# A two-layer diffusion trunk on one core: the retention branch's own products by seven block products, and its last gate put behind the first Fourier projection

## Chip, cores and metric

One core of one Trainium2 chip. The metric is the device time of one launch in microseconds (us), lower is better.

## What is computed

The reference runs two layers over 640 tokens (512 noisy ones and 128 of a prompt, each group with its own modulation). A layer projects the normalised input once, has three branches (retention, latent attention, Fourier mixing), and merges them:

```
h = rms_norm(x, norm_g) * (1 + scale) + shift
rq, rk, rv, rz, q_lat, kv_lat, k_r, mz, fu, fz, gl = split(h @ w_in)
...
branches = [o_r * silu(rz), o_m * silu(mz), o_f * silu(fz)]      # each 512 wide
proj     = branches[n] @ w_branch[n]                             # 512 x 1024, n = 0, 1, 2
merged   = sum over n of proj[n] * sigmoid(gl[n])                # gl: 3 x 1024 columns of h @ w_in
x        = x + gate * (merged @ w_out)
```

Every f32 operand is kept as two tiles, a rounded high part and the rest, and each product is three matmuls (high x high, high x low, low x high).

## The kernel before

Channels lie on the partitions and the 640 tokens on the free axis, in two halves of 320. PE is TensorE, DVE VectorE, ACT ScalarE, POOL GpSimd; SP issues most DMAs. Instructions are written in program order, and a scheduler sorts those of each engine into a fixed queue by its own estimate of times; each engine then works through its queue in order.

A layer has these stages: attention; retention (`retention`, four heads, whose `Filler` computes silu of the gate columns between the heads' own matmuls); Fourier mixing (`fourier`); the merge; the output projection. Three things matter here.

**Retention's last gate.** For each head `norm(hd)` transposes the head's output (L787), takes means and variances on DVE (L789, L790), a power on POOL, one more DVE operation (L795), and five scalings on ACT (L798). `gate(hd)` has the silu values finished by the filler (`rz.finish`, matmuls L319 in the one `fill` bank of PSUM, emptied by ACT's tanh L321 and DVE's L322), transposes back (L807) and multiplies on DVE (L808). `norm(3)` and `gate(3)` are the last lines of `retention`. `fourier` then starts with `sums(k)` (DVE and ACT prepare the sums of hidden columns) and `project(0)`, the first Fourier projection, 120 matmuls of 256 columns (L85 to L87).

**The merge.** Three passes n = 0, 1, 2 work on latent attention (`omt`), retention (`ort`) and Fourier (`ort` again, loaded from `ofd` in pass 1). A pass has four blocks i of 256 output channels. A block first computes the gate's columns with `seven` (a 2 x 2 block product by seven products in place of eight; 84 matmuls of 320 columns), then the branch's own product. In passes 0 and 2 that is `seven` again (42 matmuls). In pass 1 it is `four`, the plain product: 48 matmuls. `seven` needs its operand as seven sums, the parts p0 to p6, which `branch_sums` makes on DVE and ACT: eleven DVE operations of 640 elements a pass, four of them sums made in place in the source, seven of them the low half of a part, in tiles `bq0` to `bq9` and `bql`. `four` needs only the four quarters as they are (`branch_split`, `bq0` to `bq7`). The weights likewise: `br_weights` makes sums of them (`wsums`), `br_plain` does not. The last two products of a `seven` (`rest`) are issued inside the next one (`flush`).

**Buffers.** The tiles `bq0` to `bq9` and `bql` have one buffer each, and `wh` and `wl` have four. A pass can fill a part's tile only when the pass before has used it for the last time.

Of the kernel before, what the change touches and what calls it, by code (L numbers as in the profile page):

```python
# [9 lines left out]
F32R = mybir.dt.float32r  # L10
# [20 lines left out]
def build(nc, tc, A, O):  # L31
# [38 lines left out]
    def h2(sb):  # L70
        return sb.rearrange("p (h n) -> p h n", h=2)
# [590 lines left out]
    def retention(l, rp, orr, spare):  # L662
# [139 lines left out]
        def gate(hd):  # L802
            nn = outp[hd]
            z = rz.finish(hd + 1)
            pt = big()
            for t in range(NT):
                PE.transpose(pt[:, t * P:(t + 1) * P], nn[:, t * P:(t + 1) * P], ident)  # L807
            DVE.scalar_tensor_tensor(orr[hd], pt[:, :TT], 0.5, z, op0=ALU.mult, op1=ALU.mult)  # L808
# [23 lines left out]
        for p in todo:  # L832
            mix(*p)
        norm(3)
        gate(3)


    def fourier(l, fp, of, sums, wgp):
        def table(name, src, a, n):
            raw = fp.tile([P, a, n], F32, name="traw", tag="traw", bufs=1)  # L840
            nc.sync.dma_start(raw, src)
# [68 lines left out]
        def prompt_t(g):  # L910
# [4 lines left out]
            split(upc[0][:, g, :], upc[1][:, g, :], Up[:, 0:P], scale=1.0 / 128)  # L915
            split(ups[0][:, g, :], ups[1][:, g, :], Up[:, P:256], scale=-1.0 / 128)

        for k in range(4):
            sums(k)
        project(0)  # L920
        teo = [table(f"te{i}", A["k_dft"][i].rearrange("(a p) n -> p a n", p=P), 2, 256) for i in range(2)]
        tp_ = table("tpr", A["k_dftp"].unsqueeze(1), 1, 256)
        cf = table("tcf", A["k_dftf"].unsqueeze(1), 1, 256)
# [135 lines left out]
        g = lambda w, i: (w[0][:, s[i]], w[1][:, s[i]])  # L1059
        return g(w1, 0), g(w1, 3), g(w1, 1), g(w1, 2), g(w2, 0), g(w2, 1), g(w2, 2)  # L1060

    def br_plain(l, idx, c0):
        r = wraw(rows(A["w_branch"][l, idx], 0, 4, c0, 256), 4, 256)
        w = wtiles(4, 256)
        split(w[0], w[1], r, leng=DVE)
        return w

    def branch_split(gp, src):
        for w in range(4):
            hi, lo = (gp.tile([P, 2, 320], F32R, name=f"bq{2 * w + i}", tag=f"bq{2 * w + i}", bufs=1) for i in range(2))  # L1070
            split(hi, lo, h2(src[:, w, :]))
            yield hi, lo

    def four(ws, xs, y2, ms, ps, tick, mid=None, fin=None):
        for j in range(2):
            for h, hs in enumerate(HALF):
                A = bank()
                for k in range(4):
                    for i, (u, v) in enumerate(PASSES):
                        PE.matmul(A, ws[u][:, k, j * P:(j + 1) * P], xs[k][v][:, h, :], start=(k == 0 and i == 0),  # L1080
                                  stop=(k == 3 and i == 2))
                if not (j or h):
                    flush()
                    if mid:
                        mid()
                DVE.scalar_tensor_tensor(ps[j][:, hs], y2[j][:, hs], 1.0, A, op0=ALU.add, op1=ALU.mult)
                tick(3 * h)
                if fin:
                    DVE.tensor_tensor(ms[j][:, hs], ms[j][:, hs], ps[j][:, hs], op=ALU.add)
                    fin(j, hs)  # L1090
            if not fin:
                DVE.tensor_tensor(ms[j], ms[j], ps[j], op=ALU.add)

    tail = []

    def flush():
# [90 lines left out]
    for l in range(DEPTH):  # L1187
# [8 lines left out]
        orr = [ort[:, w, :] for w in range(4)]  # L1196
        off = [oft[:, w, :] for w in range(4)]
        with ExitStack() as s:
            retention(l, pool(s, f"re{l}"), orr, off)
        s3 = ExitStack()  # L1200
        hqp = pool(s3, f"hq{l}")
        wgp = pool(s3, f"wg{l}")
        with ExitStack() as sx:
            sums, close, hq = hidden_sums(hqp, pool(sx, f"hx{l}"), off)
            with ExitStack() as s:
                w0, gated = fourier(l, pool(s, f"fo{l}"), off, sums, wgp)
            close()
        ofd = dp.tile([P, 4, TT], F32, name=f"ofd{l}")
        for w in range(2):
# [4 lines left out]
        with ExitStack() as s:  # L1214
# [57 lines left out]
            for n, (idx, src, tmp) in enumerate(((1, omt, None), (0, ort, om), (2, ort, om))):  # L1272
                if n:
                    flush()
                parts = branch_split(gp, src) if n == 1 else branch_sums(gp, src, bql)
                np_ = 4 if n == 1 else 7
                bq = []
                for i in range(4):
                    if n and i % 2 == 0:
                        y2 = tmp[2:4]  # L1280
                    else:
                        y2 = [fl.tile([P, TT], F32, name="tg", tag="th", bufs=2) for _ in range(2)]
                    seven(gl_weights(wgp, l, C_GL + D * idx + 256 * i), hq, *y2, *gates(y2, n, bq, parts, np_))
                    if n == 2 and i == 3:
                        merge(0, 4)
                    if i == 0:
                        flush()
                        bq += list(parts)
                        if n == 1:
                            for w in range(4):  # L1290
                                nc.sync.dma_start(ort[:, w, :], ofd[:, w, :])
                    ms = [mg[2 * i], mg[2 * i + 1]]
                    ps = tmp[0:2] if n else ms
                    if n == 1:
                        ends = (lambda: merge(4, 6), lambda j, hs: merge(6 + j, 7 + j, hs)) if (n, i) == (2, 3) else ()
                        four(br_plain(l, idx, 256 * i), bq, y2, ms, ps, lambda i: next(steps, None) if i else None, *ends)
                    else:
                        seven(br_weights(wgp, l, idx, 256 * i), bq, *ps, *products(y2, n, ms, ps))
            merge(4, 6)
            flush()  # L1300
            merge(6, NK)
# [158 lines left out]
```

## Time and profile before

| | |
|---|---|
| median of 3 runs | 1472.1 us (1469.72 to 1475.49) |
| the profiled execution | 1475.04 us |
| its span on the core | 1473.3 us |
| PE busy | 96% of the span, 9793 matmuls |
| DVE busy | 70% |
| ACT, POOL busy | 51%, 16% |
| stage with the merge, layer 0 and 1 | 428 to 697 us and 1148 to 1401 us |

Times in the trace count from the start of the span. A matmul's duration overlaps the next one's, so what one costs is the distance between starts, or a stretch divided by its count. DVE's operations overlap a little too. A row with `[0.55 <-DVE th L322]` says that the engine was idle for 0.55 us before this instruction, until that operation ended.

### The profile page before, as it was taken

To read this page: it belongs to the slowest core of one execution; us is meant where nothing else is said; L and a number is where in the kernel's file an instruction comes from. 1 tells how busy PE (TensorE), PEld (TensorE's weight loads), DVE (VectorE), ACT (ScalarE), POOL (GpSimd) and SP (SyncE) were. 2 spreads that over 40 slices of the span, in tenths; PEclk is the share of its full clock that TensorE was granted. 3 is DMA by queue.
4 is the path that set the end of the run, shared out by engine and by line. 5 is a ranking of instruction groups with operands and counts; after the bars stand their busy time and mean duration, and the time that the engine had idled before them with its cause. 6 is when DMAs were issued, how large, how long until landed. Compare 5 with 4: busy or idle time off the path is not lost.

```text
span 1473.3 us, 25184 instructions
## 1 busy us (share of the span) xinstructions
PE 1411.6 (96%) x9793; PEld 1345.2 (91%) x9793; DVE 1025.5 (70%) x1896; ACT 756.2 (51%) x1607; POOL 239.1 (16%) x227
## 2 busy tenths in 40 slices
PE   6999999999999999999999999999999999999997
PEld 4989989988988989999999899899889899999997
DVE  5367776666887686698573777765759778779843
ACT  5546666544545453455354566664545445445542
POOL 1220000301102211122312100021110112112240
PEclk9999999999999999999999999999999999999999
DMA  9520003331325474233532100042222433323342
GB/s 317 179 76 1 15 16 98 102 84 33 94 90 176 130 221 129 57 85 92 166 101 84 33 15 16 15 138 77 73 73 65 146 108 104 94 80 86 90 125 87
DMA packets 175847, 138.91 MB, mean 94 GB/s; under 512 B 8304, under 2 KB 168688, under 8 KB 175728
## 3 DMA queue, kind: packets, MB, share of 16 engines
q1 hardware_dynamic: 157680, 120.16, 28.1%
q10 hardware_dynamic: 18048, 17.15, 3.7%
q8 instruction: 77, 1.26, 0.4%
q14 instruction: 42, 0.34, 0.1%
HBM read 125.98 MB, written 11.30 MB: 93 GB/s over the span
## 4 chain that ended last, share of the span: by engine, by line
PE 74%; DVE 12%; DMA 5%; ACT 4%; issue 4%; POOL 1%; SPq 0%; POOLq 0%; ACTq 0%; DVEq 0%
PE bank L1109 25%; PE sm L85 6%; PE sm L87 5%; PE sm L86 5%; PE big L269 4%; PE bank L1080 4%; PE big L513 4%; PE fill L319 3%; PE sm L319 3%; PE sm L534 2%; PE sm L526 2%; DVE wl L74 2%; PE fill L187 2%; DMA raw<-in_w_in 1%; PE big L411 1%
## 5 line engine op out<-in xcount | busy, mean ns | idle before, releaser
L74 DVE TENSOR_TENSOR wl<-raw,wh 128x1024 fp32r<-128x1024 f32 (+5 forms) x146 | 153.8, 1055 | 87.3 <-ACT wh L78 39.0
L78 ACT CAST wh<-raw 128x1024 fp32r<-128x1024 f32 (+5 forms) x126 | 104.7, 833 | 86.2 <-DMA raw<-in_w_in 27.9
L1109 PE MATMUL bank<-hh,wh 128*128 128x320 f32 x416 | 130.0, 315 | 5.5 <-ACT tg L1125 4.4
L85 PE MATMUL sm<-wh,hh 128*128 128x256 f32 (+2 forms) x456 | 134.2, 295 | 0.5 <-DVE vl L74 0.5
L86 PE MATMUL sm<-wl,hh 128*128 128x256 f32 (+2 forms) x456 | 133.8, 294 | 0.0
L87 PE MATMUL sm<-wh,hl 128*128 128x256 f32 (+2 forms) x456 | 132.6, 294 | 0.0
L1109 PE MATMUL bank<-hl,wh 128*128 128x320 f32 x416 | 128.6, 310 | 0.0
L1109 PE MATMUL bank<-hh,wl 128*128 128x320 f32 x416 | 127.1, 311 | 0.0
L74 POOL TENSOR_TENSOR wl<-raw,wh 128x1024 fp32r<-128x1024 f32 (+1 forms) x32 | 66.4, 2075 | 294.9 <-ACT wh L78 215.7
L74 POOL TENSOR_TENSOR wl<-st,wh 128x512 fp32r<-128x512 f32 x26 | 38.0, 1463 | 328.8 <-ACT wh L78 328.8
L85 PEld LDWEIGHTS sm<-wh,hh 128*128 128x128 f32 x456 | 87.8, 193 | 2.2 <-issue 0.8
L1109 PEld LDWEIGHTS bank<-hh,wh 128*128 128x128 f32 x416 | 78.3, 188 | 11.9 <-ACT tg L1125 5.2
L86 PEld LDWEIGHTS sm<-wl,hh 128*128 128x128 f32 x456 | 87.8, 193 | 0.1
L87 PEld LDWEIGHTS sm<-wh,hl 128*128 128x128 f32 x456 | 87.4, 192 | 0.4 <-issue 0.4
L1109 PEld LDWEIGHTS bank<-hl,wh 128*128 128x128 f32 x416 | 78.5, 189 | 0.0
L1109 PEld LDWEIGHTS bank<-hh,wl 128*128 128x128 f32 x416 | 78.0, 189 | 0.0
L74 DVE TENSOR_TENSOR ptl<-sm,pth 128x384 fp32r<-128x384 f32 x128 | 67.2, 549 | 13.9 <-ACT pth L78 12.9
L1109 PE MATMUL bank<-bq,wh 128*128 128x320 f32 x320 | 72.0, 311 | 0.0
L78 ACT CAST pth<-sm 128x384 fp32r<-128x384 f32 x128 | 57.2, 481 | 22.6 <-PE sm L526 21.8
L78 ACT CAST wh<-st 128x512 fp32r<-128x512 f32 x68 | 39.6, 618 | 55.1 <-PE bank L1109 53.7
L640 DVE TENSOR_REDUCE nm<-big 128x1 f32<-128x768 f32 x64 | 60.7, 948 | 1.7 <-PE big L513 1.6
L74 DVE TENSOR_TENSOR wl<-st,wh 128x512 fp32r<-128x512 f32 x42 | 40.8, 972 | 29.5 <-ACT wh L78 27.0
(578 smaller groups left out, 4540.3 us busy)
## 6 DMA issues: line engine op xcount, KB each, us to landing
raw<-in_w_in SPq DMA_DIRECT2D x96, 512.0 KB, 4.0
mraw<-in_w_mod ACTq DMA_DIRECT2D x32, 512.0 KB, 4.0
raw<-in_w_branch SPq DMA_DIRECT2D x24, 512.0 KB, 3.6
mraw<-in_w_mod SPq DMA_DIRECT2D x16, 512.0 KB, 9.2
raw<-in_w_out SPq DMA_DIRECT2D x16, 512.0 KB, 4.3
raw<-in_w_in SPq DMA_DIRECT2D x8, 384.0 KB, 6.1
om<-xd SPq DMA_DIRECT2D x16, 192.0 KB, 3.5
xd<-xt SPq DMA_DIRECT2D x8, 320.0 KB, 4.2
```

What stands on the lines that cost most here:

```text
L74: eng.tensor_tensor(lo, src, hi.bitcast(F32), op=ALU.subtract)
L78: ACT.copy(hi, src)
L85: PE.matmul(out, ah, bh, start=first, stop=False)
L86: PE.matmul(out, ah, bl, start=False, stop=False)
L87: return PE.matmul(out, al, bh, start=False, stop=last)
L187: PE.matmul(ps[c:c + 32, :n], cs[:, 2 * (j + i):2 * (j + i) + 32], rv[:, i, :], start=(j + i < 4), stop=(j + i >= 4), tile_position=(0, c))
L269: PE.matmul(ps[:, 512 * h:512 * h + 320], ws[a][:, k, :], xs[b][k][:, 320 * h:320 * h + 320], start=(first and k == 0 and i == 0), stop=(l ...
L319: PE.matmul(ps, w[a][:, k, :], (hh, hl)[b][k][:, hs], start=(k == 0 and i == 0), stop=(k == NK - 1 and i == 2))
L513: PE.matmul(S[:, 512 * h:512 * h + 384], qT[hd][a][:, t * P:(t + 1) * P], (kth, ktl)[b][hd % 3][:, 384 * h:384 * h + 384], start=(i == 0), ...
L640: DVE.tensor_reduce(nm, Sv, axis=AX.XY if len(Sv.shape) == 3 else AX.X, op=ALU.max, negate=True)
L1080: PE.matmul(A, ws[u][:, k, j * P:(j + 1) * P], xs[k][v][:, h, :], start=(k == 0 and i == 0), stop=(k == 3 and i == 2))
L1109: PE.matmul(ps, w[u], x[v], start=(first and k == 0 and j == 0), stop=(k == n - 1 and j == 2), skip_group_check=True)
```

## The change

Pass 1 now uses `branch_sums`, `br_weights` and `seven` as the other two do; `four`, `branch_split` and `br_plain` go. `retention` returns its last gate as a function, and `fourier` calls it after `project(0)`; `sums` come after both.

```diff
@@ retention
         norm(3)
-        gate(3)
+        return lambda: gate(3)
@@ fourier
+        project(0)
+        lastgate()
         for k in range(4):
             sums(k)
-        project(0)
@@ build, the merge
-                parts = branch_split(gp, src) if n == 1 else branch_sums(gp, src, bql)
-                np_ = 4 if n == 1 else 7
+                parts = branch_sums(gp, src, bql)
+                np_ = 7
...
-                    if n == 1:
-                        ends = (lambda: merge(4, 6), lambda j, hs: merge(6 + j, 7 + j, hs)) if (n, i) == (2, 3) else ()
-                        four(br_plain(l, idx, 256 * i), bq, y2, ms, ps, lambda i: next(steps, None) if i else None, *ends)
-                    else:
-                        seven(br_weights(wgp, l, idx, 256 * i), bq, *ps, *products(y2, n, ms, ps))
+                    seven(br_weights(wgp, l, idx, 256 * i), bq, *ps, *products(y2, n, ms, ps))
```

In both layers together PE has 48 matmuls of 320 columns fewer; DVE has 78 instructions more, ACT 54 and POOL 8. Line numbers of the changed kernel are lower: L1113 becomes L1082, L1258 L1227, L1010 L1011, L973 to L979 L974 to L980.

Three places show how the queues move. The first is PE's queue at the transposes of `norm(3)` in layer 0. Before:

```order
L319 MATMUL fill<-hh_156,wh 128x320
L319 MATMUL fill<-hl_164,wh 128x320
L787 MATMUL big<-ident,of 128x128 x5
L319 MATMUL fill<-hh_156,wl 128x320
L86 MATMUL sm<-wl,hh_149 128x256
L87 MATMUL sm<-wh,hl_157 128x256
```

Changed:

```order
L319 MATMUL fill<-hl_164,wh 128x320
L319 MATMUL fill<-hh_156,wl 128x320
L787 MATMUL big<-ident,of 128x128 x5
L319 MATMUL fill<-hh_149,wh 128x320
L319 MATMUL fill<-hl_157,wh 128x320
L319 MATMUL fill<-hh_149,wl 128x320
```

Between L787 and the gate's transposes L807 there were one filler matmul and 23 of the projection; now there are 24 of the filler, its last half, right behind its first half. The projection's matmuls moved ahead of L787.

The second is DVE's queue at the same place, from the head's statistics on. Before:

```order
L789 BN_STATS st_4248<-big 128x6 x5
L790 BN_AGGR mv<-st_4248 128x2
L74 TENSOR_TENSOR wl<-raw,wh 128x1024
L790 BN_AGGR mv<-st_4248 128x2 x2
L322 SCALAR_TENSOR_TENSOR th<-th,fill 128x320
L790 BN_AGGR mv<-st_4248 128x2 x2
L795 SCALAR_TENSOR_TENSOR nm_4266<-mv,rs_4265 128x5
L974 TENSOR_TENSOR hx_4359<-of 128x320
L974 TENSOR_TENSOR hx_4360<-of 128x320
L808 SCALAR_TENSOR_TENSOR or<-big,th 128x640
```

Changed:

```order
L322 SCALAR_TENSOR_TENSOR th<-th,fill 128x320
L789 BN_STATS st_4248<-big 128x6 x5
L790 BN_AGGR mv<-st_4248 128x2 x5
L795 SCALAR_TENSOR_TENSOR nm_4266<-mv,rs_4265 128x5
L975 TENSOR_TENSOR hx_4291<-of 128x320
L975 TENSOR_TENSOR hx_4292<-of 128x320
L974 TENSOR_TENSOR of<-hh_154,hl_162 128x640
L976 TENSOR_TENSOR of<-of 128x320
L74 TENSOR_TENSOR wl<-raw,wh 128x1024
L322 SCALAR_TENSOR_TENSOR th<-th,fill 128x320
```

The weight's low half and the filler's L322 no longer stand inside the statistics; the filler's first-half L322 now stands ahead of them, and four operations of `sums` stand between L795 and the gate, where two did.

The third is DVE's queue where pass 2 of layer 0 makes its parts. Before, in pass 1, ahead of its last operations on DVE (three of them are L1086, the first of which is the last row):

```order
L74 TENSOR_TENSOR bq1_7066<-or_2999,bq0_7065 128x640
L74 TENSOR_TENSOR bq5_7070<-or_2999,bq4_7069 128x640
L1010 TENSOR_TENSOR or_2999<-or_2999 128x2x320
L74 TENSOR_TENSOR wl_7100<-raw_7075,wh_7099 128x1024
L74 TENSOR_TENSOR bq7_7072<-or_2999,bq6_7071 128x640
L1013 TENSOR_TENSOR or_2999<-or_2999 128x2x320
L74 TENSOR_TENSOR bq3_7068<-or_2999,bq2_7067 128x640
L74 TENSOR_TENSOR wl_7220<-st_7227,wh_7219 128x512
L1113 TENSOR_TENSOR tg_6876<-bank_6946,tg_6876 128x320
L1086 SCALAR_TENSOR_TENSOR om_165<-tg_6875,bank_7021 128x320
```

Changed, behind the operation that takes product 5 of pass 1's last block from PSUM (L1227 on bank_7037), from the 16th instruction after it:

```order
L74 TENSOR_TENSOR bql_5212<-or_2999,bql_5212 128x640
L1232 SCALAR_TENSOR_TENSOR om_165<-om_165 128x320
L1011 TENSOR_TENSOR or_2999<-or_2999 128x2x320
L74 TENSOR_TENSOR wl_7337<-raw_7332,wh_7336 128x1024
L1082 TENSOR_TENSOR om_165<-bank_7204,om_165 128x320
L74 TENSOR_TENSOR bq7_7128<-or_2999,bq6_7127 128x640
L1014 TENSOR_TENSOR or_2999<-or_2999 128x2x320
L74 TENSOR_TENSOR wl_7339<-st_7343,wh_7338 128x512
L1025 TENSOR_TENSOR raw_7332<-raw_7332,raw2_7334 128x512
L1026 TENSOR_TENSOR raw_7332<-raw_7332,st_7343 128x512
L74 TENSOR_TENSOR bq3_7124<-or_2999,bq2_7123 128x640
L1023 TENSOR_TENSOR st_7456<-raw_7446 128x256
```

`bq1` and `bq5` are the low halves of p0 and p2, `bq3`, `bq7` and `bq9` those of p1, p3 and p5; `wl_7337` belongs to the gate of pass 2's second block. Before, most parts of pass 2 were made before pass 1 had ended; now all but p0 and p2 are made after product 5 of its last block, since that product reads `bq8` and `bq9`.

## Rows read from the trace of the kernel before

**Rows 1.** The page: busy time, share of the span and instructions of each engine.

```profile
PE 1411.6 (96%) x9793; PEld 1345.2 (91%) x9793; DVE 1025.5 (70%) x1896; ACT 756.2 (51%) x1607; POOL 239.1 (16%) x227
```

**Rows 2.** Windows, layer 1, one block of pass 1, one of pass 2.

```profile
core 0: us, PE busy (x) PEld busy (x) DVE busy (x) ACT busy (x) POOL busy (x), PEclk, DMA share, GB/s
1294.96:1314.32 19.36, 19.36 (x135) 19.36 (x133) 12.93 (x18) 7.54 (x12) 2.60 (x2) 1.00 0.31 82
1354.21:1372.69 18.48, 18.48 (x128) 18.48 (x127) 16.82 (x27) 9.38 (x18) 4.38 (x3) 1.00 0.21 58
```

**Rows 3.** Windows, same columns: passes 1 and 2 of layer 0; layer 1; their border there.

```profile
544.80:697.20 152.40, 151.84 (x1053) 147.38 (x1050) 118.11 (x180) 72.55 (x130) 29.85 (x20) 1.00 0.33 92
...
1256.20:1333.60 77.40, 77.40 (x530) 77.40 (x529) 57.06 (x79) 34.13 (x57) 14.88 (x9) 1.00 0.28 75
1333.60:1401.40 67.80, 67.25 (x459) 66.98 (x458) 60.54 (x95) 37.51 (x71) 15.36 (x11) 1.00 0.31 87
...
1323.00:1333.50 10.50, 10.50 (x73) 10.50 (x73) 10.50 (x15) 7.78 (x14) 4.84 (x2) 1.00 0.22 56
```

**Rows 4.** Timeline of PE at retention's last gate: start, duration, instruction; layer 0, then 1.

```profile
369.98 0.71 PE L787 MATMUL big<-ident,of 128*128 128x128 f32 x5
...
373.30 0.28 PE L87 MATMUL sm<-wh,hl 128*128 128x256 f32 x1
376.21 1.87 PE L807 MATMUL big<-ident,of 128*128 128x128 f32 x5 [2.63 <-ACT of L798]
377.87 0.58 PE L85 MATMUL sm<-wh,hh 128*128 128x256 f32 x1
...
1096.24 1.87 PE L807 MATMUL big<-ident,of 128*128 128x128 f32 x5 [2.63 <-ACT of L798]
```

**Rows 5.** Windows just behind that gate.

```profile
378.00:382.00 4.00, 4.00 (x27) 4.00 (x27) 3.88 (x8) 2.68 (x8) 0.52 (x1) 0.75 0.74 187
...
386.00:420.00 34.00, 32.74 (x255) 31.72 (x254) 32.23 (x71) 17.93 (x46) 2.58 (x4) 1.00 0.26 70
```

**Rows 6.** Timeline of ACT and DVE between the transposes of rows 4.

```profile
370.73 1.09 DVE L789 BATCH_NORM_STATS2 st<-big 128x6 f32<-128x128 f32 x5 [3.45 <-PE big L787]
...
371.82 1.19 DVE L74 TENSOR_TENSOR wl<-raw,wh 128x1024 fp32r<-128x1024 f32 x1
...
375.70 1.85 ACT L798 ACTIVATE of<-big,nm,rs 128x128 f32<-128x128 f32 x5 [4.13 <-DVE nm L795]
```

**Rows 7.** Timeline: PE waits for the filler's bank, an earlier head.

```profile
339.56 0.41 PE L319 MATMUL fill<-hh,wh 128*128 128x320 f32 x1 [0.55 <-DVE th L322]
```

**Rows 8.** Timeline: PE waits for DVE in the Fourier transforms, layer 0.

```profile
413.66 0.39 PE L87 MATMUL sm<-te1h,fw 128*128 128x256 f32 x1 [0.56 <-DVE fw L74]
```

**Rows 9.** Groups by line and shape, DVE: count, busy us, mean ns, idle before.

```profile
L74 DVE TENSOR_TENSOR wl<-raw,wh 128x1024 fp32r<-128x1024 f32 x100 | 123.1, 1233 | 80.2 <-ACT wh L1033 32.5 <-ACT wh L78 32.0 <-ACT wh L1043 15.0
...
L74 DVE TENSOR_TENSOR wl<-st,wh 128x512 fp32r<-128x512 f32 x42 | 40.8, 972 | 29.5 <-ACT wh L78 27.0 <-PE fill L187 2.5
...
L1113 DVE TENSOR_TENSOR om<-bank,om 128x320 f32<-128x320 f32 x48 | 22.7, 480 | 1.2 <-PE bank L1109 0.6 <-ACT om L1131 0.6
...
L1265 DVE TENSOR_TENSOR mg<-mg,om 128x640 f32<-128x640 f32 x16 | 19.5, 1217 | 0.2
...
L74 DVE TENSOR_TENSOR bq<-or,bq 128x640 fp32r<-128x640 f32 x18 | 15.9, 891 | 1.1 <-ACT bq L78 1.0
```

**Rows 10.** Timeline of DVE: two operations in a row, pass 1 of layer 1.

```profile
1324.99 0.81 DVE L1010 TENSOR_TENSOR or<-or 128x640 f32<-128x640 f32 x1
1325.73 1.21 DVE L74 TENSOR_TENSOR wl<-raw,wh 128x1024 fp32r<-128x1024 f32 x1
```

**Rows 11.** Timeline: a POOL subtraction, a DVE operation beside it, one of that shape alone.

```profile
1342.63 1.29 POOL L74 TENSOR_TENSOR wl<-st,wh 128x512 fp32r<-128x512 f32 x1 [10.62 <-ACT wh L78]
...
1342.79 1.41 DVE L1022 TENSOR_TENSOR st<-raw 128x256 f32<-128x256 f32 x1
...
1351.58 0.41 DVE L1024 TENSOR_TENSOR raw<-raw 128x256 f32<-128x256 f32 x1
```

More of the change, by code (lines that the diff above doesn't have):

```diff
@@ L834, in retention, with fourier @@
         norm(3)
-        gate(3)
-    def fourier(l, fp, of, sums, wgp):
+        return lambda: gate(3)
+    def fourier(l, fp, of, sums, wgp, lastgate):
         def table(name, src, a, n):
@@ L1060, in br_weights @@
         return g(w1, 0), g(w1, 3), g(w1, 1), g(w1, 2), g(w2, 0), g(w2, 1), g(w2, 2)
[L1062 to L1092, printed above, removed]
     tail = []
@@ L1198, in build @@
         with ExitStack() as s:
-            retention(l, pool(s, f"re{l}"), orr, off)
+            lastgate = retention(l, pool(s, f"re{l}"), orr, off)
         s3 = ExitStack()
@@ L1205, in build @@
             with ExitStack() as s:
-                w0, gated = fourier(l, pool(s, f"fo{l}"), off, sums, wgp)
+                w0, gated = fourier(l, pool(s, f"fo{l}"), off, sums, wgp, lastgate)
             close()
```

## Prediction, made blind

> **What bounds the kernel now.** I read the page first: PE is busy for 1411.6 of the span's 1473.3 us (96%), DVE for 70% [rows 1]. So work taken from PE counts, and work added elsewhere costs only where PE has to wait for it. The windows say where that could be. A block of pass 1 lasts 19.36 us with PE busy for all of it, one of pass 2 18.48 us in the same way [rows 2]. In passes 1 and 2 of layer 1 PE is busy for 77.40 of 77.40 and 67.25 of 67.80 us, but DVE for 57.06 and 60.54, far above its 70% [rows 3]. At the border of these passes there are 10.5 us in which DVE too has no gap, and PE still doesn't wait [rows 3]: there PE is the limit, and DVE is next behind it. The timeline at retention's last gate shows the other thing that the change touches, PE idle while the head's normalisation runs through DVE, POOL and ACT [rows 4, 6].
>
> The profiled execution took 1475.04 us, 2.9 above the median of 1472.1; I make the sum against the former and carry its difference to the median. A measurement of this kernel tells about 0.5%, 7.4 us, from no change.
>
> **PE's matmuls.** Six matmuls fewer in each of 4 blocks and 2 layers are 48. A slot of 320 columns is 18.48 us / 126 = 0.1467 us, and 132 of them give pass 1's 19.36 [rows 2]. 48 x 0.1467 = **-7.0 us**. All of it lies in a stretch where PE never waits, so it counts in full unless a new wait eats it.
>
> **Retention's gate.** Before, PE starts the transposes L787 at 369.98, has filled the wait with one matmul of the filler and 23 of the projection by 373.4, idles to 376.21, and then the five transposes L807 take 1.66 us to the next start at 377.87, since ACT delivers their inputs one by one (1.85 us for five) [rows 4, 6]. From 369.98 to 377.87 are 7.89 us. Behind it PE's granted clock is 0.75 for 4 us, which is another 1.0 us; it has just been idle [rows 5]. After, 24 filler matmuls stand between L787 and L807, 24 x 0.147 = 3.5 us. They need the single `fill` bank, which ACT and DVE must empty of the first half; for such a turn PE waited 0.55 us at an earlier head [rows 7]. Transposes (0.47 by 5 slots of 0.094, as its record of 0.71 overlaps the next), wait and matmuls end 4.6 us after L787's start. The normalisation now took 5.72 us from L787 to L798 (369.98 to 375.70); a weight's low half inside it (371.82 to 372.92, 1.10) and one L322 (0.4, a shape of 0.48 in rows 9) go out, and one L322 ahead of the statistics comes in (0.4 at most). That leaves about 4.65 to L798, 5.15 to L807 and 6.8 to its end [rows 4, 6]. So 1.1 us is saved on these 7.9, and the stretch holds 0.6 us more of work than before (3.5 against 2.9): 1.7, or 2.7 if the clock does not fall. Layer 1 has the same 2.63 us wait at 1096.24 [rows 4]. Against that: what follows is short of DVE. From 386 to 420 DVE is busy for 32.23 of 34 us, and PE waits for its `fw` at 413.66 [rows 5, 8]. DVE gets the projection's results no sooner, and four operations of `sums` now stand ahead of the gate; its queue to the last `fw` can be 1.0 us later, which with the 0.8 us that DVE gains ahead is a loss of 0.2. Between 0.2 lost and 2.6 gained I take 1.1, nearest to the middle, as PE's idle shows but DVE's share limits: **-2.2 us** for two layers, ends +0.4 and -5.2.
>
> **DVE at the borders.** The parts p1 and p3 to p6 use tiles that the pass before reads to its last block's product 5 (`bq8`, `bq9`), so they, and what stands behind them in DVE's queue, can only follow the DVE operation on that product's bank (L1227). Before, pass 1 had no such part and pass 2 made most of its own early. No row shows this; I bound it. In the changed queue I add up DVE's operations from that L1227 to the first tile that PE needs, with the mean of each shape (0.48 for 320 elements, 0.81 to 1.22 for 640, 0.97 for 512 on `wl`, 1.23 for 1024, 0.41 for 256) [rows 9 to 11], each less 0.07, because one of 0.81 is followed after 0.74 [rows 10]. Against that stands what PE has to do between, at 0.1467 a matmul, less 0.45 for the hand-over to DVE and back, an estimate: a matmul's record is 0.26 longer than its slot [rows 7], DVE starts 0.04 after it [rows 4, 6], and the way back is taken as 0.15.
> - Layer 0, into pass 1: 16 operations, 10.5 us, against 11.4 on PE (61 matmuls, and 18 small ones): no wait.
> - Layer 0, into pass 2: 19 operations (four of 320 make 1.6, eight of 640 7.2, three of 512 2.25, three of 256 1.1, one of 1024 1.2), 13.3 us, against 75 matmuls, 11.0: wait 13.3 + 0.45 - 11.0 = 2.8.
> - Layer 1, into pass 1: 17 operations, 11.3, against 76 matmuls, 11.15: wait 0.6.
> - Layer 1, into pass 2: 24 operations to the low half of p1, 17.0, against 109 matmuls, 16.0: wait 1.5.
>
> Together **+4.9 us**. With the shortest durations of each shape only layer 0's second place stays, 0.7. At the other end one operation in each of the four is held up by POOL: a POOL subtraction runs from 1342.63 for 1.29 us, and a DVE operation of 256 elements beside it takes 1.41 instead of the 0.41 of such a one alone, 1.0 more [rows 11]. Then the four waits are 0.6, 3.8, 1.6 and 2.5, together 8.5. I take the means, because they hold the usual share of such delays. The high halves of parts and weights on ACT and the low halves on POOL I cost at nothing as long as DVE's queue is the later one: ACT is busy for 37.51, POOL for 15.36 of pass 2's 67.80 [rows 3]. Without that cover they would be late by their own few tenths.
>
> The Trainium skill has a rule on this ("SBUF — State Buffer", section "Who interferes with whom"): a DVE instruction with two inputs in SBUF contends with a GpSimd instruction that reads SBUF, and whoever came first holds the shared ports for its whole length. The pair in rows 11 agrees, at 1.41 against 0.41. The change adds eight POOL subtractions, so by this rule every border should be priced at the upper end, and the sum would be -0.7 where mine is -4.3.
>
> Sum: -7.0 - 2.2 + 4.9 = **-4.3**; 1475.04 - 4.3 = 1470.7 for such an execution, and 2.9 less for the median, **1467.8 us**.
>
> **Rivals.**
> - *The parts come in time.* The waits are 0.7 or less in all: -7.0 - 2.2 + 0.7 = -8.5, 1463.6; with the gate's full gain -11.5, 1460.6. For it: the gapless 10.5 us of DVE without a wait of PE [rows 3], and my sums of means carry idle that overlaps. Against: the added DVE operations stand in front of the first tiles of the pass. Faster.
> - *POOL holds DVE at each border*: -7.0 - 2.2 + 8.5 = -0.7, 1471.4. For: the pair in rows 11. Against: POOL is busy for a fifth of these passes only [rows 3]. Within 0.5%.
> - *The gate's move gives nothing.* L807 still has 24 matmuls ahead of it as before, and what PE does not wait for there it waits for at `fw` [rows 8]: -7.0 + 4.9 = -2.1, 1470.0.
> - *DVE becomes the bound of passes 1 and 2: slower.* Per layer the change adds about 22 us to DVE there: 12 operations that take a bank's 320 elements (0.41, 4.9), seven more on parts (0.74, 5.2), 16 sums of weights with 256 elements, twelve of them as if alone (0.34, 4.1) and the four of L1022 as beside POOL (1.34, 5.4) [rows 11], and some 2.5 for low halves of weights. In layer 1 DVE has 57.06 + 60.54 = 117.6 of 145.2 us; 139.6 would be 96%. It decides once DVE idles more than 4% of the time. If it idles as in pass 2 (1 - 60.54/67.80 = 10.7%), the two passes last 139.6/0.893 = 156.3 instead of 145.2, +11.1; layer 0, with 118.1 of 152.4, +4.5 [rows 3]. These replace both the -7.0 and the +4.9: 15.6 - 2.2 = +13.4, 1485.5. For: DVE's share, and PE's wait where DVE is at 95% [rows 5, 8]. Against: 10.50 of 10.50 without any idle [rows 3], so DVE can run gapless.
>
> **How the numbers follow.** Chances: my forecast 0.40, the parts in time 0.30, POOL at each border 0.08, the gate without gain 0.10, DVE as the bound 0.12. Faster by over 0.5% (below 1464.7) are the second case and 0.04 of the first, by a gate at its best: 0.34. Slower (above 1479.5) is the last: 0.12. The rest is 0.54. The range begins at 1460.5, the second case with the full gate. At the top the forecast's own unfavourable ends, -7.0 + 0.4 + 8.5 = +1.9, give 1474.0; I take it on to 1477, which holds the mildest part of the last case, a quarter to a half of its +13.4, and leaves about 0.15 outside on both sides.
>
> **What would show it.** Right: 9745 matmuls; blocks of pass 1 at 18.5 us; waits of PE on `wl`, `bq` or `bql` at the first block of pass 2 in layer 0 (near 2.8 us) and less in layer 1; DVE at 93 to 97% of passes 1 and 2; the wait ahead of the last L807 below 1 us, and a new one of some 0.6 before the second half's filler. Wrong: waits of PE in blocks 1 to 3 of these passes (DVE as the bound), no wait at the borders (parts in time), or the gate's gain coming back as waits for `fw`.

## The result, and the profile after

The changed kernel took 1487.16 us (median, 1484.10 to 1490.71) against 1472.19 us of the kernel before: a ratio of 1.0107, 95% interval 1.0087 to 1.0128. It is **slower by 1%**, where I forecast 0.3% faster. A second comparison, further down, gave 1.0093 (1.0071 to 1.0115). The profiled execution after took 1484.10 us with a span of 1482.2.

The page after, busy times and the chain's shares:

```profile
PE 1410.6 (95%) x9745; PEld 1339.7 (90%) x9745; DVE 1058.0 (71%) x1974; ACT 776.3 (52%) x1661; POOL 263.7 (18%) x235
PE 70%; DVE 13%; DMA 6%; ACT 5%; issue 5%; POOL 1%; SPq 0%; POOLq 0%; ACTq 0%; DVEq 0%
```

On the chain that ended last PE's share is 70%, and the rest went to what PE waited for. The 48 matmuls are gone, yet the span is 8.9 us longer: PE's idle time went from 61.7 to 71.6 us. PE is also busy for only 1.0 us less than in [rows 1], not 7.0: a matmul's record is 0.31 us or more for a slot of 0.147, so the first part of each wait counts as busy, and parts of either execution ran at a lower granted clock. Where PE waits more, the passes tell. First passes 1 and 2 of layer 0, then of layer 1, in the profile before, each from its first matmul to the next pass's (the span, then PE, PE's loads, DVE, ACT, POOL busy, the granted clock, DMA):

```profile
537.10:622.30 85.20, 85.20 (x608) 80.36 (x607) 57.26 (x85) 33.81 (x56) 10.11 (x8) 1.00 0.41 116
622.30:697.10 74.80, 74.25 (x505) 73.84 (x505) 67.34 (x105) 42.72 (x81) 20.50 (x13) 1.00 0.31 87
1249.30:1326.60 77.30, 77.30 (x529) 77.30 (x528) 56.41 (x78) 33.43 (x54) 11.34 (x8) 1.00 0.32 87
1326.60:1401.40 74.80, 74.25 (x507) 73.98 (x506) 67.54 (x105) 42.44 (x80) 20.20 (x13) 1.00 0.31 87
```

The same after:

```profile
539.30:621.50 82.20, 82.20 (x587) 77.60 (x586) 73.61 (x118) 42.97 (x83) 18.39 (x12) 1.00 0.43 126
621.50:702.50 81.00, 76.61 (x505) 74.66 (x505) 74.23 (x112) 44.49 (x83) 22.05 (x13) 0.99 0.31 86
1253.20:1329.40 76.20, 74.37 (x505) 73.84 (x504) 67.96 (x108) 41.38 (x79) 23.26 (x13) 1.00 0.37 101
1329.40:1410.50 81.10, 76.34 (x506) 73.99 (x505) 73.26 (x114) 45.15 (x83) 22.14 (x13) 1.00 0.30 82
```

Pass 1 got 3.0 us shorter in layer 0 and 1.1 in layer 1. Pass 2, whose matmuls did not change, got 6.2 and 6.3 us longer. (These borders are good to some 0.3 us. Counted strictly, each pass's matmuls back from the last one of the merge, the four passes took 85.6, 74.9, 77.4 and 74.7 us before and 82.2, 81.0, 76.3 and 81.1 after: 7.9 us more in all.) PE now idles for 4.4 and 4.8 us in pass 2, where it idled for 0.55, and for 1.8 us in layer 1's pass 1; that is as much as the 9.9 us by which its idle time grew.

Three places hold most of it. **The border of the passes.** PE, layer 0, the start of pass 2; then DVE and ACT there:

```profile
632.93 0.41 PE L1078 MATMUL bank<-bql,wh 128*128 128x320 f32 x1 [0.88 <-ACT bql L78]
633.87 0.42 PE L1078 MATMUL bank<-hh,wh 128*128 128x320 f32 x1 [0.54 <-ACT wh L1034]
637.79 0.42 PE L1078 MATMUL bank<-hh,wl 128*128 128x320 f32 x1 [0.57 <-DVE wl L74]
...
625.00 0.47 DVE L1227 SCALAR_TENSOR_TENSOR om<-tg,bank 128x320 f32<-128x320 f32 x1
...
626.52 1.52 DVE L74 TENSOR_TENSOR wl<-st,wh 128x512 fp32r<-128x512 f32 x1 [0.19 <-ACT wh L78]
...
631.30 0.81 DVE L1009 TENSOR_TENSOR or<-or 128x640 f32<-128x640 f32 x1
...
632.15 0.72 ACT L78 CAST bql<-or 128x640 fp32r<-128x640 f32 x1 [2.14 <-DVE or L1009]
```

From L1227 at 625.00 to L1009 at 631.30 DVE has ten operations and but one gap, of 0.19 us. ACT then waits 2.14 us for L1009, and PE for ACT. With what each wait costs beyond its bracket (a matmul of 0.147 us starts 1.19 us after the one ahead of it, where the bracket says 0.88), the three are 1.04, 0.80 and 0.73 us, 2.6 together, and 2.8 with the slot after each, which is 0.1 us longer. Two of the three waits end with ACT: it has to cast `bql` (0.72) and then the gate's weight (1.04), and could not start before L1009. In layer 1 the waits are these:

```profile
1264.91 0.41 PE L1078 MATMUL bank<-hh,wh 128*128 128x320 f32 x1 [0.89 <-ACT wh L1034]
1277.70 0.42 PE L1078 MATMUL bank<-hh,wh 128*128 128x320 f32 x1 [0.94 <-ACT tg L1094]
...
1341.15 0.41 PE L1078 MATMUL bank<-bql,wh 128*128 128x320 f32 x1 [0.50 <-ACT bql L78]
1342.09 0.42 PE L1078 MATMUL bank<-hh,wh 128*128 128x320 f32 x1 [0.53 <-ACT wh L1034]
```

The last two are as in layer 0: ACT waited 1.83 us for L1009 before it cast `bql` and the weight. The first two, in pass 1, are not. ACT's cast of the weight (1.04) waited 0.57 us for a matmul of L1078, as far as the rows tell for one of the four `wh` buffers; a block of pass 1 now takes five of their turns where it took four. And the copy `tg` came late after DVE had waited 1.19 us for a subtraction of POOL that took 4.25. Pass 2 of layer 1 has three more waits, of 0.20 us ahead of these and of 0.62 and 0.49 a block later. In brackets the waits in the first 28 us of a pass, the border's from here on, sum to 6.2 us, and in a second profile of the same kernel, further down, to 6.2 again.

**The end of pass 2.** The last blocks' copies on ACT, after, and PE's wait for them; then ACT before:

```profile
698.34 1.04 ACT L78 CAST wh<-raw 128x1024 fp32r<-128x1024 f32 x1 [1.67 <-DMA raw<-in_w_out]
699.29 0.42 ACT L1100 COPY om<-bank 128x320 f32<-128x320 f32 x1
...
699.77 0.57 PE L1078 MATMUL bank<-bq,wh 128*128 128x320 f32 x2 [1.90 <-ACT om L1100]
...
1408.65 0.56 PE L1078 MATMUL bank<-bq,wh 128*128 128x320 f32 x2 [2.07 <-ACT om L1100]
```

```profile
694.20 0.42 ACT L1131 COPY om<-bank 128x320 f32<-128x320 f32 x1
695.73 1.05 ACT L78 CAST wh<-raw 128x1024 fp32r<-128x1024 f32 x1 [1.10 <-DMA raw<-in_w_out]
```

Before, the cast of the output projection's third weight, which waits for its load, stood behind the copy that PE needs. After, it stands ahead, so PE waits for a DMA that it doesn't use yet. No line of the code there was changed; ACT's order was, which the scheduler makes from its own estimate of times.

**The gate.** PE and ACT at retention's last gate, layer 0, after:

```profile
368.97 0.71 PE L787 MATMUL big<-ident,of 128*128 128x128 f32 x5
370.18 0.42 PE L319 MATMUL fill<-hh,wh 128*128 128x320 f32 x1 [0.50 <-DVE th L322]
373.98 1.72 PE L807 MATMUL big<-ident,of 128*128 128x128 f32 x5
376.91 0.39 PE L85 MATMUL sm<-wh,hh 128*128 128x256 f32 x1 [1.20 <-ACT un L855]
...
373.47 1.85 ACT L798 ACTIVATE of<-big,nm,rs 128x128 f32<-128x128 f32 x5 [3.87 <-DVE nm L795]
375.19 1.06 ACT L78 CAST wh<-raw 128x1024 fp32r<-128x1024 f32 x1
376.13 0.46 ACT L321 ACTIVATE th<-fill 128x320 f32<-128x320 f32 x1
376.46 0.94 ACT L855 COPY un<-sm 128x256 f32<-128x256 f32 x3
```

The 2.63 us wait of [rows 4] is gone. But a weight's cast and a tanh now stand between L798 and the copies `un` that empty the projection's banks, and PE waits 1.20 us for these: from L787 to the next projection matmul are 7.94 us, where there were 7.89 before. Further on the mean granted clock is 0.58 from 412 to 424 us (its lower level, 1.2 GHz, for most of that stretch), in the Fourier transforms, where PE waited for DVE and ACT four times from 410 us on; in the kernel before it was 1.00 there, with three such waits:

```profile
412.00:424.00 12.00, 10.46 (x46) 9.60 (x46) 7.45 (x24) 4.12 (x14) 0.30 (x3) 0.58 0.15 45
```

### The profile page after: what moved, and what is told of

Read it like the earlier page. It is cut to its first block, busy times and chain, and to the rows that moved or that the text cites. A ratio compares the mean times of both kernels' runs of the same rounds, so it can differ in the third digit from the quotient of the medians.

```text
span 1482.2 us, 25255 instructions
## 1 busy us (share of the span) xinstructions
PE 1410.6 (95%) x9745; PEld 1339.7 (90%) x9745; DVE 1058.0 (71%) x1974; ACT 776.3 (52%) x1661; POOL 263.7 (18%) x235
## 4 chain that ended last, share of the span: by engine, by line
PE 70%; DVE 13%; DMA 6%; ACT 5%; issue 5%; POOL 1%; SPq 0%; POOLq 0%; ACTq 0%; DVEq 0%
PE bank L1078 24%; PE sm L85 6%; PE sm L87 6%; PE sm L86 6%; PE big L513 4%; PE big L269 3%; PE fill L319 3%; PE sm L319 3%; PE sm L534 2%; DVE wl L74 2%; DMA raw<-in_w_in 2%; PE sm L526 2%; PE fill L187 1%; PE big L411 1%; DMA ofd<-of 1%
## 5 line engine op out<-in xcount | busy, mean ns | idle before, releaser
L78 ACT CAST wh<-raw 128x512 fp32r<-128x512 f32 (+4 forms) x142 | 109.0, 774 | 99.4 <-DMA raw<-in_w_in 29.8
L1078 PE MATMUL bank<-hh,wh 128*128 128x320 f32 x416 | 130.4, 314 | 7.1 <-ACT tg L1094 4.7
L74 POOL TENSOR_TENSOR wl<-raw,wh 128x512 fp32r<-128x512 f32 (+1 forms) x40 | 75.1, 1880 | 332.7 <-ACT wh L78 259.8
L1078 PE MATMUL bank<-hl,wh 128*128 128x320 f32 x416 | 128.1, 309 | 0.0
L1078 PE MATMUL bank<-hh,wl 128*128 128x320 f32 x416 | 126.9, 310 | 0.6 <-DVE wl L74 0.6
L1078 PE MATMUL bank<-bq,wh 128*128 128x320 f32 x480 | 108.6, 312 | 4.9 <-ACT om L1100 4.0
L74 POOL TENSOR_TENSOR wl<-st,wh 128x512 fp32r<-128x512 f32 x26 | 53.1, 2041 | 303.7 <-ACT wh L78 296.2
L1078 PEld LDWEIGHTS bank<-hh,wh 128*128 128x128 f32 x416 | 78.1, 188 | 13.8 <-ACT tg L1094 5.5
L1078 PEld LDWEIGHTS bank<-bq,wh 128*128 128x128 f32 x480 | 79.6, 188 | 9.3 <-ACT om L1100 4.5
L1078 PEld LDWEIGHTS bank<-hh,wl 128*128 128x128 f32 x416 | 77.6, 188 | 1.4 <-DVE wl L74 1.0
L1078 PEld LDWEIGHTS bank<-hl,wh 128*128 128x128 f32 x416 | 78.1, 188 | 0.0
L74 DVE TENSOR_TENSOR ptl<-sm,pth 128x384 fp32r<-128x384 f32 x128 | 67.3, 549 | 13.8 <-ACT pth L78 12.7
L1078 PE MATMUL bank<-bq,wl 128*128 128x320 f32 x240 | 72.5, 310 | 0.0
L74 DVE TENSOR_TENSOR wl<-st,wh 128x512 fp32r<-128x512 f32 x50 | 56.7, 1133 | 12.8 <-ACT wh L78 12.8
```

The costliest lines, as they stand in the source:

```text
L74: eng.tensor_tensor(lo, src, hi.bitcast(F32), op=ALU.subtract)
L78: ACT.copy(hi, src)
L1078: PE.matmul(ps, w[u], x[v], start=(first and k == 0 and j == 0), stop=(k == n - 1 and j == 2), skip_group_check=True)
```

## The experiments

**One part of the change alone.** The theory (A) is that several places add up: borders, the end of pass 2, the gate. The main rivals are that DVE's load bounds the merge throughout (B), or that the gate is all (C). The first kernel takes only the merge's part of the change, the second only the gate's:

```diff
# merge alone: the changed kernel with
-        return lambda: gate(3)
+        gate(3)
...
-        project(0)
-        lastgate()
         for k in range(4):
             sums(k)
+        project(0)
```

> Only the merge's part of the change (pass 1 by seven products); retention's gate and the Fourier stage as before. Theory A (several places): 7.0 us less of matmuls, waits of some 6.6 us at the borders of the passes, and 4.3 us, with a clock loss of up to 1.7, at the end of pass 2, where a weight's cast that waits for its DMA stands ahead of a copy on ACT: together 4 to 6 us over the kernel before, about 1477. Theory B (the merge's DVE load alone is the cause): the whole of the change's loss, +13 to +16, about 1486 to 1488. Theory C (the gate's move is the whole loss): -7 to -4, about 1466.

> Only the gate's part: pass 1 of the merge stays the plain product. Theory A: from the gate to the merge's first matmul layer 0 takes 3.6 us more (waits in the Fourier transforms and a granted clock of 0.5 behind them), layer 1 the same as before, or 5 more too where its clock falls as well: +3 to +10, about 1476 to 1482. Theory B: 0 within 2 us. My forecast's step (the gate's move gains): -2 to -5.

The merge alone: 1483.04 us against 1471.70, ratio 1.0075 (1.0057 to 1.0094), 11 us slower. The gate alone: 1475.45, ratio 1.0024 (1.0012 to 1.0035), 3.7 us slower. Both parts lose, and together they make the whole loss of the first comparison: 11.3 + 3.7 = 15.0 (the second comparison has 13.0). C falls, and so does the step of my forecast by which the gate's move gains. The merge lies between A's number and B's; in its profile pass 2 is 5.1 and 7.2 us longer than before (1.7 of the 7.2 is clock), and PE waits 1.93 and 1.83 us for L1099's copy (L1100 of the changed kernel), with the gate as it was. So the end of pass 2 belongs to the merge's part. In the profile of the gate alone passes 1 and 2 are as before, and from L787 to the merge's first matmul are 60.2 us in both layers, where the two profiles of the kernel before have 58.1 to 58.6; the granted clock cost each of these stretches the same 1.7 us.

**The cast put back.**

```diff
-        ACT.copy(y2[:, b], A)
+        ends[:] = [ACT.copy(y2[:, b], A)]
...
-                if d < 4:
+                if d == 2:
+                    with tc.issue_after(ends[0].ins):
+                        ws.append(wload(view, NK, P, eng))
+                elif d < 4:
```

> The changed kernel, with one edit: on ACT the third cast of the output projection's weights is queued behind the last copy of the merge's last block, as it is before the change. Theory A: the waits of 2.06 and 2.23 us of PE for that copy go, with the clock loss of 1.7 us behind one of them: 4 to 6 us less than the changed kernel, about 1482. Theory B: DVE or the load is late anyway, so the wait moves to the next matmuls and the time stays within 1 us of the changed kernel's.

It took 1483.20 us, ratio 1.0079 (1.0057 to 1.0100), 4.0 less than the changed kernel's 1487.16, but 1.6 less than the median of all its ten executions (1484.8, with the second comparison), which is within their scatter. The windows are sharper: pass 2 lasts 78.9 and 79.5 us instead of 81.0 and 81.1, 3.7 less in all. The end of pass 2, layer 0, now:

```profile
693.28 0.56 PE L1078 MATMUL bank<-bq,wh 128*128 128x320 f32 x2 [0.42 <-ACT om L1094]
694.94 0.56 PE L1078 MATMUL bank<-bq,wh 128*128 128x320 f32 x2 [0.52 <-ACT om L1100]
...
694.46 0.43 ACT L1100 COPY om<-bank 128x320 f32<-128x320 f32 x1 [1.23 <-PE bank L1078]
694.78 1.05 ACT L78 CAST wh<-raw 128x1024 fp32r<-128x1024 f32 x1
```

The wait of 1.90 is 0.52, and that of 2.07 in layer 1 is 0.52 too. Theory A's place is shown by these, at 3.7 us for both layers, of which 0.9 was clock behind the wait of layer 0; the executions' times don't show it.

**The parts' tiles rotated.** Part p5 and the rest go into the tiles that the pass before gives up first, so that none has to wait for product 5.

```diff
+        if turn:
+            old = list(home)
+            for p, q in zip((0, 5, 1, 2, 3, 4, 6), (0, 2, 1, 4, 3, 5, 6)):
+                home[p] = old[q]
...
-            hi, lo = t[2 * i:2 * i + 2]
+            hi, lo = t[2 * at[i]:2 * at[i] + 2]
```

> The changed kernel, with the parts of each pass put into the tiles in the order in which the pass before gives them up, so that no part waits for product 5 of the last block; same operations, no tile more. Theory A: the border waits of 6.6 us shrink to 1 or 2: 4 to 6 us less than the changed kernel, about 1482. Theory B: DVE's sum of work sets the passes, the same operations are only done earlier or later: within 1.5 us of the changed kernel.

1484.49 us, ratio 1.0086 (1.0070 to 1.0102): no less than the median of the changed kernel's ten. PE at the same border:

```profile
627.13 0.41 PE L1087 MATMUL bank<-hq1h,wl 128*128 128x320 f32 x1 [1.32 <-DVE wl L74]
633.52 0.56 PE L1087 MATMUL bank<-bq,wh 128*128 128x320 f32 x2 [1.02 <-ACT wh L78]
```

The parts are early, and a weight's low half (`wl`) is late in their stead, 1.32 us. The border's waits don't shrink: 7.0 us in brackets, after 6.2. By its number B was right. But the DVE operations just ahead of this `wl` are longer than elsewhere, since they now fall on POOL's subtractions:

```profile
621.15 1.51 DVE L74 TENSOR_TENSOR bq<-or,bq 128x640 fp32r<-128x640 f32 x1
622.59 1.51 DVE L1032 TENSOR_TENSOR st<-raw 128x256 f32<-128x256 f32 x1
624.02 1.92 DVE L1023 TENSOR_TENSOR or<-or 128x640 f32<-128x640 f32 x1
...
621.95 1.87 POOL L74 TENSOR_TENSOR w<-raw,w 128x512 fp32r<-128x512 f32 x1
623.78 1.48 POOL L74 TENSOR_TENSOR wl<-raw,wh 128x512 fp32r<-128x512 f32 x1
```

Alone such operations take 0.81, 0.41 and 0.81 us [rows 10, 11], so 2.9 us are added, more than the wait. This run therefore does not separate DVE's own work from POOL's hold on it; a run further down, with low halves moved from POOL to DVE, comes back to this.

**Less for DVE, in two ways.** One kernel leaves the low halves of p3, p4 and p6 out in passes 1 and 2 (the high half takes their place in the products), the other has POOL make them. The second one's edit; the first has `None` in place of `POOL`:

```diff
-            yield place(3, B(0, 1), DVE)
-            yield place(4, B(1, 1), DVE)
+            yield place(3, B(0, 1), POOL if n else DVE)
+            yield place(4, B(1, 1), POOL if n else DVE)
...
-            yield place(6, B(1, 0), DVE)
+            yield place(6, B(1, 0), POOL if n else DVE)
```

> The changed kernel without the low halves of the parts p3, p4 and p6 in passes 1 and 2 (their place in the products is taken by the high halves, so the same number of matmuls): 12 DVE operations of 640 elements fewer in all, three in the queue at each of four borders. Theory A (DVE's queue at the borders, 0.8 us an operation): of the 6 to 8 us of waits there 5 to 7 go, 1480 to 1482 beside the changed kernel's 1487. Theory B (the waits hang on the load and cast of weights, not on DVE's queue): within 1.5 us of the changed kernel. Theory C (DVE bounds both passes throughout): 9 us or more, each operation at its full 0.8.

> The changed kernel with the same three low halves of passes 1 and 2 made by POOL instead of DVE. Theory A: half of what leaving them out gives, 2 to 4 us less than the changed kernel, as POOL is busy for a quarter of these passes. Theory D (POOL's operations hold DVE up for their length, as in the pair of rows 11, 1.0 us each): nothing gained or up to 6 us more than the changed kernel.

Left out: 1483.49 us, ratio 1.0061 (1.0045 to 1.0077). By the windows its passes 1 and 2 sum to 317.4 us (82.6, 78.8, 75.2, 80.8) against 320.5 after; counted strictly, as above, to 319.0 against 320.6. That is 1.6 to 3.1 less for 12 operations of 0.8 us, 9.7. So DVE doesn't bound the passes throughout (C of that expectation falls). A's 5 to 7 was too much as well: the border's waits went from 6.2 to 3.9 in brackets, since these operations come behind the L1009 for which ACT, and with it PE, waits first.

Made by POOL: **1499.74 us**, ratio 1.0181 (1.0168 to 1.0194), 12.6 us more than the changed kernel (14.9 more than the median of its ten). Not even the upper end that I gave to theory D reaches it. POOL and DVE at the start of pass 1, layer 1:

```profile
1268.92 1.56 POOL L74 TENSOR_TENSOR bql<-or,bql 128x640 fp32r<-128x640 f32 x1 [5.46 <-ACT bql L78]
1272.00 1.74 POOL L74 TENSOR_TENSOR bq<-or,bq 128x640 fp32r<-128x640 f32 x1 [1.52 <-ACT bq L78]
...
1269.14 2.02 DVE L1010 TENSOR_TENSOR or<-or 128x640 f32<-128x640 f32 x1
...
1272.22 2.59 DVE L74 TENSOR_TENSOR wl<-raw,wh 128x1024 fp32r<-128x1024 f32 x1
```

L1010 takes 2.02 us where it takes 0.81 alone, and the next 2.59 where its mean is 1.23 [rows 9, 10]: these two POOL operations cost DVE 1.2 and 1.4 us, more than the 0.8 that each takes off it, and beside each of the other ten a DVE operation grew too, by 0.5 to 1.4. At some 0.5 us net that is 6 us for twelve, half of the loss; PE's waits in the passes went from 11.0 to 19.3 us in brackets, and the rest was not taken apart. The Trainium skill has the rule ("SBUF — State Buffer", section "Who interferes with whom"): a DVE instruction with two inputs in SBUF contends with a GpSimd instruction that reads SBUF, for ports that are locked exclusively. The trace agrees: both POOL operations started 0.22 us ahead, and L1010 ended 0.68 us after the first of them.

**The gate with its cast put back.** On ACT, the next projection's weight is cast behind the `un` copies:

```diff
             if ch:
+                with tc.issue_after(copied[2].ins):
+                    lead = [next(columns)]
...
-                    ACT.copy(un[t], ps)
+                    copied.append(ACT.copy(un[t], ps))
```

> Only the gate's part of the change, as in the gate-only run, with one edit: on ACT the cast of the second projection's first weight is queued behind the three copies that empty the first projection's banks, not ahead of them. Theory A: the 1.2 us that PE waits for these copies in each layer go and the transforms behind them are earlier: 2 to 4 us less than the gate alone, 1471.5 to 1473.5, no better than before. Theory B (the gate's loss is the transforms' waits for DVE, which has four more operations ahead): 1475 to 1476 as with the gate alone.

1472.96 us, ratio 1.0006 (0.9995 to 1.0016): most of the gate's loss of 3.7 us is gone, 0.7 is left (the two intervals overlap a little), and its gain still does not come. PE and ACT of that kernel, layer 0:

```profile
370.35 0.41 PE L319 MATMUL fill<-hh,wh 128*128 128x320 f32 x1 [1.16 <-DVE th L322]
373.97 0.71 PE L807 MATMUL big<-ident,of 128*128 128x128 f32 x5
406.51 0.39 PE L85 MATMUL sm<-tprh,uph 128*128 128x256 f32 x1 [1.28 <-DVE ul L82]
410.21 0.38 PE L85 MATMUL sm<-te1h,fh 128*128 128x256 f32 x1 [1.44 <-ACT fh L78]
416.22 0.87 PE L85 MATMUL big<-uh,tcfh 128*128 128x256 f32 x2 [0.62 <-ACT uh L81]
...
373.64 0.94 ACT L859 COPY un<-sm 128x256 f32<-128x256 f32 x3
374.42 2.06 ACT L78 CAST wh<-raw 128x1024 fp32r<-128x1024 f32 x2
```

The 2.63 us at the gate have become 1.16 there and 1.28, 1.44 and 0.62 in the transforms, where the two profiles of the kernel before have waits of 1.2 and 0.7 us in all. The inputs that PE waits for there are made by DVE and ACT, and DVE has no gap from 374.7 us to behind 410.

**The kernel before, once more.**

> The kernel before, a second profile, unchanged. Theory A: the profile that the forecast was read from, 3 us above the median, holds waits for loads of the modulation weights in pass 0 that other executions don't have; a typical one is 1471 to 1473 with passes 1 and 2 as long as there (within 0.5 us each). Theory B: passes 1 and 2 themselves vary by over 2 us from execution to execution.

1471.47 us, span 1469.7; passes 1 and 2 last 85.4, 74.9, 77.3 and 74.8 us, the same as in the first profile within 0.2. So the differences by pass hold, and the profile that I forecast from was 3.6 us longer elsewhere.

**Edits together, and the changed kernel again.** The first of these has both casts put back, the second the merge alone with its cast and the rotated tiles, the third beside that one low half of branch weights a block on DVE in place of POOL, the last no edit:

```diff
# third kernel, in br_weights
-        split(w1[0][:, 0:4], w1[1][:, 0:4], r[:, :, c1], leng=POOL)
+        split(w1[0][:, 0:4], w1[1][:, 0:4], r[:, :, c1], leng=DVE)
```

> The changed kernel with both casts on ACT put back behind the copies (the edits of the cast-back run and of the gate-cast run together). Theory A (two separate places in ACT's queue): the gains add, 4.0 and 2.5, so 6 to 7 us less than the changed kernel, 1479.5 to 1482, 8 to 10 over the kernel before: what is left is the border of the passes and the clock. Theory B (one cause behind both): 4 us or less. With the transforms' waits shorter, the clock losses in the Fourier stage of 5 to 7 us are gone and the executions scatter less, by 5 us or less.

> The merge's part alone with the cast put back and the parts' tiles rotated; the gate as before. Theory A: 1483 (merge alone) less 4 for the cast and 2.7 for the tiles: 1475 to 1478, still slower than the kernel before, since three waits of 1 to 2 us at the borders now hang on weights' low halves. Theory B (the border is gone with the tiles, only the tail of clock losses is left): 1472 or less.

> As the run with the merge alone, cast and tiles, with the one low half of each block's branch weights that POOL made (128 x 512) made by DVE: 24 POOL operations fewer, 24 of DVE more. Theory D (a POOL operation costs DVE as much time as it would take DVE to do it): within 1.5 us of that run, as 24 x 0.6 us more of DVE's work stand against some 1.0 us of delay each. Theory A (DVE's queue is what is short at the borders): 2 to 4 us more than that run.

> The changed kernel, unchanged, a second profile and more executions. Theory A: 1484 to 1490 in two groups by the granted clock, 5 us apart: with one or with two layers whose Fourier transforms run at a clock of 0.5; passes 1 and 2 within 0.5 us of the first profile. Theory B: the scatter comes from waits for loads, and the clock is the same in all.

Both casts: 1481.34 us, ratio 1.0065 (1.0044 to 1.0085); 3.5 less than the ten's median of 1484.8, 5.8 less than the first one of 1487.16. Together the two places give something, less than the 6 to 7 expected. The scatter did not shrink (1477.8 to 1485.7). The merge with cast and tiles: 1484.22, ratio 1.0084 (1.0064 to 1.0105), a miss: 6.7 less than the merge alone was expected, and it is no faster. Counted strictly, its passes sum to 319.0 us against 318.1 with the cast alone, so the tiles give nothing, as above; the border's waits are 6.7 us in brackets. With 24 low halves on DVE in place of POOL: 1480.74, ratio 1.0063 (1.0044 to 1.0082), 3.5 less, though the intervals overlap and the passes are longer (322.4, 1.7 of it clock). Its time settles nothing, but its waits say more: at the borders 2.5 us in brackets are left of 6.7, and PE's 1.33 us for the `wl` in layer 0 is gone. One POOL subtraction fewer falls on DVE's operations there, and the scheduler also put the part behind this `wl`; the run does not tell the two apart, and neither of its theories had them. In place of those waits PE waits for `wl` further inside the passes (1.29, 1.93 and 0.49 us), where DVE has more to do. The changed kernel again: 1484.76 (1483.23 to 1491.99), passes within 0.4 us of the first profile; its executions form no two groups. In this profile the transforms ran at full clock in both layers, in the first one at 0.58 in layer 0, and in that of the run with fewer low halves, which took 1488.48 us, at 0.6 in both:

```profile
412.00:424.00 12.00, 10.22 (x47) 9.37 (x48) 7.58 (x23) 4.29 (x15) 0.30 (x3) 0.63 0.15 45
1139.00:1152.00 13.00, 11.29 (x50) 10.14 (x51) 8.36 (x25) 4.55 (x16) 0.30 (x3) 0.62 0.13 42
```

That is up to 5 us a layer (12 x 0.37 and 13 x 0.38), and it comes and goes from execution to execution of one kernel. Neither of the two profiles of the kernel before shows it. No version here beats the kernel before.

## Why the prediction was wrong, step by step

Three steps of the sum failed: the gate was followed only to the end of L807, ACT's casts at the borders were costed at nothing, and the end of pass 2 stood in no term. What the runs show in place of the forecast's -7.0 - 2.2 + 4.9 is -7.0 + 3.7 + 9.0 + 5.8 = +11.5.

- **PE's matmuls, -7.0: right.** There are 9745, and pass 1 of layer 0, which had no new wait at its start, got 3.0 us shorter by the windows and 3.4 by strict count, of its 3.5.
- **Gate, -2.2: wrong; alone it measured +3.7.** The step that failed is "5.15 to L807 and 6.8 to its end", from which 1.1 us was taken as saved. The wait for the head went as worked out (0.50 where I had 0.55; L798 4.50 us behind L787 where I had 4.65; L807's end at 6.73 where I had 6.8), but L807's end is not where the next projection starts. Behind it PE needs ACT's `un` copies, and ACT's queue there had changed: 7.94 us, none saved. I had even written that DVE's share limits the gain and set the low end at a loss of 0.2 a layer. The rival "the gate's move gives nothing" was the right one for its mechanism: with the cast put back, nothing is what it gives, and new waits stand in the transforms.
- **Borders, +4.9: right in place, short in size, right only in part in mechanism.** In distances between starts, beyond 0.147 us a matmul, the borders cost 9.0 us: 2.8 in pass 2 of layer 0 where I had 2.8, 2.4 against 0.6 and 3.9 against 1.5 in layer 1, and none in pass 1 of layer 0, as forecast. DVE's queue was added up well: its 19 operations into layer 0's pass 2 took 12.7 us of 13.3, the 17 into layer 1's pass 1 11.2 of 11.3. The step that failed is "The high halves of parts and weights on ACT and the low halves on POOL I cost at nothing": 5.1 of the 6.2 us in brackets end with an operation of ACT. 2.45 of these are for its two casts behind L1009 (0.72 and 1.04), 0.9 for the cast that waited for its buffer, a term that I had not priced and that no run here undoes alone, and the rest, most of it 25 us behind the border, for copies and casts that the delayed DVE work delays in turn. Nor is it the tiles' release alone that makes the parts late: with the tiles rotated the waits stay, and only in the run that also takes low halves off POOL, with another order of DVE's queue, do they fall to 2.5. How much of them is the release, DVE's own work or POOL's hold is therefore not shown. In the hand-over of 0.45 the way back, 0.15, had no row behind it; in layer 0 PE starts 0.06 us after the end of the `bql` cast (632.15 + 0.72).
- **The end of pass 2, not in my sum at all.** I read the order of the queues only where the diff adds or moves operations. This place has none; by starts it cost 5.8 us, 0.9 of them clock, and the run that undoes the cast's move took back 3.7.
- **Sum for passes 1 and 2.** -7.0 + 9.0 + 5.8 = +7.8; the passes, counted strictly, have +7.9. So nothing of size is left over there.
- **The rival that DVE becomes the bound** gave 1485.5, near the result, but not by its mechanism: DVE's share of passes 1 and 2 is about 90% and not 93 to 97, PE is busy all through pass 1 of layer 0, and 9.7 us less of DVE's work made the passes only 1.6 to 3.1 shorter. Its closeness is luck: it has +15.6 for the passes where +7.9 were measured, and -2.2 for the gate where +3.7 were.
- **POOL at each border**: the `wl` behind L1227 took 1.52, 1.37 and 1.00 us at the three borders with waits, each beside a POOL subtraction, where the shortest of its shape take 0.68. That is 1.9 us of DVE's time there. The run with low halves on POOL shows the price where it is raised; the one with low halves taken off POOL has shorter waits at the borders, with another order of DVE's queue beside it.

What stays open: the +11.5 stand against 15.0 us in the first comparison and 13.0 in the second. The mean granted clock of ten executions after is 0.9914, that of 45 before 0.9927, which is 0.0013 x 1480 = 1.9 us more, 0.9 of it perhaps counted above. The rest is within the scatter of either kernel, and why the clock falls in some executions and not in others is not shown.

## What to carry to other kernels

When a scheduler orders the queues, a change moves rows where the code did not change. Compare every queue over the whole stage and look for an operation that now stands ahead of one that the bounding engine needs, above all one that waits on a DMA; here two casts had moved so, one of them behind a load, and undoing both took back 3.5 to 5.8 us of the loss. And before trading PE's work for DVE's, look at the border at which DVE must prepare what comes next: a mean share of 74% in a pass [rows 3] said nothing of the 6.3 us at the border in which the changed kernel's DVE had one gap of 0.19 us, nor of the casts that ACT had to do behind it. Time saved ahead of a stage that waits for DVE comes back as waits inside it.

## What was not expected of the hardware

A subtraction on POOL was no relief for DVE here: twelve of 128 x 640 moved there cost 12.6 us, and a DVE operation beside one grew from 0.81 to 2.02 us. It seems to go both ways: a subtraction of 128 x 512 on POOL, 1.29 us in [rows 11], took 4.25 us at 1269.41 in the changed kernel, beside DVE's operations, and DVE then waited 1.19 us for it. A few waits of under 1 us each in the Fourier transforms (0.65, 0.73, 0.32, 0.49 us in brackets) were at times followed by some 12 us at a mean granted clock of about 0.6, most of it at the lower level of 1.2 GHz, 5 us lost, and at times by none, in the same kernel; that is more than the waits themselves. Executions of the kernel before at a mean clock of 0.995 took 1470.8 us (three of them), at 0.990 1475.0 (two).
